# New addresses, 256-wide products, a fixed start order and the first head's rotation moved: a two-layer transformer trunk in split fp32

## The chip, the cores and the metric

The kernel runs on one core of a Trainium2 chip. The metric is the time of one execution on the device, in microseconds. Before the change it is 1125.92, the median of 3 runs (1125.34 to 1126.84).

## The reference, cut to what matters

Two trunk layers over 512 latent tokens of 1024 channels, with a context prefix of 256 tokens that only the first layer reads:

```python
for i in range(DEPTH):                                    # 2 layers
    sh1, sc1, g1, sh2, sc2, g2 = adaln_params(c, mod_w[i], mod_b[i])
    h = modulate(rms_norm(x, norm_g[i, 0]), sh1, sc1)
    if i % 2 == 0:    # 4 global heads (q and k normalised, rotated) and 4 windowed heads with a sink
        y, _ = attention_mixers(h, hc, w_in, w_out, q_g, k_g, sink, cos, sin, False)
    else:             # Fourier mixing over tokens and 4 groups of channels, then a linear map
        y = fourier_mix(h) @ fourier_w_out
    x = x + g1 * rms_norm(y, norm_g[i, 1])
    h = modulate(rms_norm(x, norm_g[i, 2]), sh2, sc2)
    x = x + g2 * rms_norm(conv_ffn(h, ...), norm_g[i, 3])   # d_ff = 2816, gated, depthwise conv of width 3
```

`adaln_params` is silu(c) times a 1024 x 6144 matrix. `apply_rope` multiplies each half of a head's channels by cosines and sines and adds them crosswise. Everything is float32.

## The kernel before, in words

**Numbers.** x stays transposed, [128 channels, 8 blocks of channels, 512 tokens]. A product in fp32 is made of three matmuls of type fp32r: each operand is split into a high part (ScalarE's copy to fp32r) and the rest (VectorE's subtraction), both on L127 in `split`. `mm3` then issues high x high (L104), high x low (L105) and low x high (L106). The pairs have two-letter names: `hh, hl` the modulated x, `wh, wl` a ring of five buffers for weights, `ch, cl` the context, `th, tl` the transposed probabilities, `qh, ql` a head's transposed queries, `xh, xl` and `zh, zl` the operands of the FFN and, in the helper `beside`, weights as well. `lhsT` is the operand held in the array as weights, `rhs` the one that moves through it, of 256 or 512 columns. `raw` is a ring of three buffers that DMAs on SyncE's queue fill.

**Addresses.** Each tile takes its bytes of a partition from a pool in the order of allocation, so a small tile ahead of another moves that one's address. `beside` puts 16 elements ahead of its weights and 16 behind.

**Order.** Work is written as Python code that calls generators (`pump(rest, n)` lets one advance by n steps); a scheduler orders the instructions of each engine by priority, which is the order of issue unless `later(n)` shifts it (a negative number is earlier). `follow(i, j)` fixes that i comes after j on its engine.

**The start (0 to 66.5 us).** The DMAs fill in the order in which they are issued: the first half of x, mod_s tile 0, constants, `w_kva` tile 0, mod_s tile 1, the second half of x, then the other tiles. The string `START` is the order in which the blocks are written: `M` (`mod_tile`) multiplies the conditioning vector by one of eight tiles mod_s and transposes the result; `W` splits weights; `X` sums squares of the second half of x; `F` (`feed`) normalises a block of x and multiplies it into the first projection of keys and values; `Y2`, `R2` normalise the context; `B0` is a filler, matmuls whose result nobody reads (`busy`, their numbers in `HOT`). The norm of the first half is spread inside `M0`, that of the second inside `M2`.

**Projections (66.5 to 112) and attention (112 to 255).** After `START` come three groups: `kb` and `vb` (the other keys and values, three blocks of tokens each) and `qa` (the queries of heads 0 and 1, two blocks). The other three groups of queries (`queries`, PSUM tile `gm`) are mixed into attention, `FILL` saying how many steps go where. `q_out` hands a block to `roped`, the rotation:

```python
def roped(dst, src, t0, gcol, stats=None, last=G):
    eng = V if gcol is None else last
    # squares on ScalarE; V: g = src * gqk; V: stats = reduce_sum(squares)
    # eng: t2 = crosswise src * sines, two halves (L814)
    # V: dst = src * cosines (L818);  last: dst = dst + t2 (L820)
```

`eng` and `last` are GpSimd for three query blocks of the first two groups; the block of heads 0 and 1 with the last tokens, (`qi == 0 and t0`), is on VectorE. The groups without a norm (`gcol is None`) multiply on VectorE and add on GpSimd. `queries_t` transposes a head's rotated queries (L998) and splits them; attention starts with `queries_t(0)`, and 12 steps of the next projection are placed behind it. GpSimd also normalises the probabilities P (L1053), which are transposed on L969.

**The rest.** Output projection (to about 318), first FFN (to 682), Fourier layer (to 765) and second FFN. Blocks of the FFNs in `SEVEN` are done by seven products of half size (256 columns), in `y_mm`; the other up projections (`up_mm`) and some of the down products are 512 wide.

Of the kernel before, what the change touches and what calls it, by code (L numbers as in the profile page):

```python
# [10 lines left out]
F32 = mybir.dt.float32  # L11
# [8 lines left out]
P = 128  # L20
# [32 lines left out]
SIDE = 16  # L53

WARM = 36
HOT = [5, 8, 5, 0]
# [3 lines left out]
START = ("M0 W0 X0 M1 B0 W1 F00 X1 F10 M2 F01 W2 F11 F20 M3 Y2 W3 F21 M4 R2 F30 F31 F02 W4 F12 F22 F32 M5 W5 F40 "  # L60
         "F41 M6 F42 W6 F50 F52 W7 F60 M7 F62 F51 F61 F70 F71 F72")
# [20 lines left out]
def kernel(ctx: ExitStack, tc: tile.TileContext, a):  # L82
# [17 lines left out]
    def f(ap):  # L100
        return ap.bitcast(F32)
# [24 lines left out]
    def split(h, l, src, eng=V):  # L126
        i = S.copy(out=h, in_=src), eng.tensor_tensor(out=l, in0=src, in1=f(h), op=ALU.subtract)  # L127
        for j in i:
            held(j)

# [8 lines left out]
    def wpair(shape):  # L139
        return mk(wp, shape, F32R, "wh", 5), mk(wp, shape, F32R, "wl", 5)  # L140
# [4 lines left out]
    con = mk(cp, [P, K_ALL], F32, "con")  # L145
    xT = mk(cp, [P, KC, T], F32, "xT")
    yT = mk(cp, [P, KC, T], F32, "yT")
    hh = mk(cp, [P, KC, T], F32R, "hh")
    hl = mk(cp, [P, KC, T], F32R, "hl")
    ident = con[:, K_ID:K_ID + P]  # L150
    ones32 = mk(cp, [P, 32], F32, "ones32")
    V.memset(ones32, 1.0)
    scol = mk(cp, [P, 2, KC], F32, "scol")
    eps = mk(cp, [P, 1], F32, "eps")
    once = mk(cp, [P, 1], F32, "once")
    mk(cp, [P, 8], F32, "cpad")
# [45 lines left out]
    def rstd(ps):  # L202
        w = ps.shape[1]
        v, t, r = (mk(cp, [P, W4], F32, "st_" + c, n)[:, :w] for c, n in (("v", 2), ("t", 1), ("r", 2)))
# [142 lines left out]
    class Plain:  # L347
# [5 lines left out]
        def tiles(self, ys, h, l, gi, pps, am, urgent=False, eng=None, pe=False):  # L353
            hs = halves[h]
            ps = ys.sums(pps, h)
# [10 lines left out]
            for k in range(KC):  # L366
# [5 lines left out]
                S.activation(out=hh[:, k, hs], in_=x, func=AF.Copy, scale=am[:, k:k + 1])  # L372
                V.scalar_tensor_tensor(out=hl[:, k, hs], in0=x, scalar=am[:, k:k + 1], in1=f(hh[:, k, hs]),  # L373
# [204 lines left out]
    with ExitStack() as es:  # L578
# [27 lines left out]
        with ExitStack() as e1:  # L606
# [30 lines left out]
            SY.dma_start(out=con, in_=a["con"])  # L637
# [29 lines left out]
            def mod_tile(c, mid=None):  # L667
# [8 lines left out]
                if mid is not None:  # L676
                    mid()
# [28 lines left out]

            ch = mk(pj, [P, KC, TC], F32R, "ch")
            cl = mk(pj, [P, KC, TC], F32R, "cl")

            tiles = [(hh, hl, t, 2 + t) for t in range(TT)] + [(ch, cl, t, t) for t in range(2)]  # L710
            sets = [(hh, hl, xT, halves[0]), (hh, hl, xT, halves[1]), (ch, cl, cT, slice(0, TC))]
# [4 lines left out]
            def feed(c, i):  # L716
# [5 lines left out]
                for n in range(2 * i, 2 * i + 2):  # L722
# [4 lines left out]
                    if (c, i) != (0, 1):  # L727
                        mm3(acc[n], sh[:, c, tk], sl[:, c, tk], wh[:, c % 2, :], wl[:, c % 2, :], c == 0, c == KC - 1)
                if (c, i) == (0, 1):

                    busy(warm, Rs[1], HOT[2])
                    for part in range(2):
                        for n in (2, 3):
                            sh, sl, t, b = tiles[n]
                            tk = slice(t * P, (t + 1) * P)
                            if part == 0:
                                PE.matmul(acc[n], lhsT=sh[:, c, tk], rhs=wh[:, 0, :], start=True, stop=False)
                                PE.matmul(acc[n], lhsT=sh[:, c, tk], rhs=wl[:, 0, :], start=False, stop=False)
                            else:
                                PE.matmul(acc[n], lhsT=sl[:, c, tk], rhs=wh[:, 0, :], start=False, stop=False)  # L740
                        if part == 0:
                            busy(warm, f(hh[:, 0, halves[1]]), HOT[3])

# [14 lines left out]

            for s in START.split():
                n = [int(c) for c in s[1:]]  # L760
                if s == "M0":
                    mod_tile(0, lambda: bcast(0, ps0))
                elif s == "M2":
                    mod_tile(2, lambda: bcast(1, Rs[1]))
                elif s == "Y2":
                    r2 = rstd(x_sums(cT, TC)[:, :W4])
                elif s == "R2":
                    Rs[2] = spread(r2, pps)
                elif s == "B0":
                    busy(warm, Rs[0], HOT[1])  # L770
                else:
                    {"M": mod_tile, "W": weights, "X": sums, "F": feed}[s[0]](*n)
# [23 lines left out]
            def roped(dst, src, t0, gcol, stats=None, last=G):  # L796
# [11 lines left out]
                if stats is not None:  # L808
                    V.reduce_sum(out=stats, in_=sq.rearrange("p (a d) -> p a d", d=P), axis=AX.X)
                t2 = mk(cp, [P, T], F32, "sq", 2).rearrange("p (t c) -> p t c", t=2)[:, :n, :]  # L810
# [9 lines left out]
                last.tensor_tensor(out=dst, in0=dst, in1=t2, op=ALU.add)  # L820

            kst = mk(pj, [P, 6, 2], F32, "kst")
# [51 lines left out]
            def q_out(qi, t0, ps):  # L874
                dst = Q[:, t0:t0 + 2, qi * 256:(qi + 1) * 256]
                if qi < 2:

                    roped(dst, ps, t0, 0, qst[:, qi, t0:t0 + 2, :].rearrange("p a b -> p (a b)"),
# [908 lines left out]
```

## Time and profile before

| | |
|---|---|
| time, median of 3 runs | 1125.92 us (1125.34 to 1126.84) |
| profiled execution | 1127.14 us, of which the profile's span is 1125.4 |
| mean clock granted to TensorE | 0.992 |
| TensorE busy (PE) | 1094.6 us, 97% of the span, 7798 matmuls |
| VectorE (DVE) | 901.9 us, 80% |
| ScalarE (ACT) | 593.6 us, 53% |
| GpSimd (POOL) | 148.9 us, 13% |
| DMA | 155.83 MB, mean 138 GB/s |

How to read the rows below. A row of instructions begins with the start in us from the span's start and the duration in us, then engine, line (that of the helper where one is used), operation, out<-in by the program's names, shapes and, after `x`, how many equal records the row covers. PE is the matmul, PEld the loading of its weights, which overlaps PE. A matmul's duration reaches to its modelled end and overlaps the next one's; the distance between two starts is the pace. A row of waits reads engine, tile and line that waited, `<-` what released it, then the sum in us, the count and the longest. In a group of instructions the three numbers after the count are the shortest, mean and longest in ns.

### The profile page before, as it was taken

The numbers are of one execution on the slowest core, as the hardware profiler recorded it, in microseconds if no ns is written. First come the engines' busy times: TensorE is split into PE (matmuls) and PEld (weight loads), VectorE is DVE, ScalarE is ACT, GpSimd is POOL, SyncE is SP. The second block draws the span as 40 slices with busy tenths as digits, with TensorE's granted clock in tenths as the row PEclk, the third lists the DMA queues.
The fourth block names the chain that finished last, engine by engine and source line by source line (L and its number), as shares of the span: only waits on it lengthen the run. The fifth ranks groups of instructions, "written<-read, shape, count | busy, mean of one in ns | idle before, by whom it ended". The sixth has DMA issues, their size and how long they took to land. (4 is left out here: it accounts for less than half of the span.)

```text
span 1125.4 us, 19521 instructions
## 1 busy us (share of the span) xinstructions
PE 1094.6 (97%) x7798; PEld 962.3 (86%) x7798; DVE 901.9 (80%) x1490; ACT 593.6 (53%) x1058; POOL 148.9 (13%) x161
## 2 busy tenths in 40 slices
PE   9999899999999999999999999989999999999995
PEld 5799888869898978887998998979888898899995
DVE  5788877764889966978999588878997998979756
ACT  4452456665675623552555445648745654655433
POOL 0047323412420000000000132400000000000012
PEclk9999999999999999999999998999999999999998
DMA  9775100172242465436525301921205523322332
GB/s 366 279 259 187 38 13 27 75 299 113 77 169 93 169 222 198 173 122 238 188 76 206 122 21 37 285 92 76 88 35 186 183 96 111 104 101 87 103 146 75
DMA packets 33763, 155.83 MB, mean 138 GB/s; under 512 B 3460, under 2 KB 8196, under 8 KB 22024
## 3 DMA queue, kind: packets, MB, share of 16 engines
q1 hardware_dynamic: 32520, 150.39, 36.9%
q0 software_dynamic: 1152, 4.19, 1.5%
q8 instruction: 61, 1.00, 0.4%
q14 instruction: 30, 0.25, 0.1%
HBM read 148.28 MB, written 6.29 MB: 137 GB/s over the span
## 5 line engine op out<-in xcount | busy, mean ns | idle before, releaser
L127 ACT CAST wh<-raw 128x1024 fp32r<-128x1024 f32 (+2 forms) x207 | 190.7, 932 | 165.1 <-PE mm L105 115.9
L127 DVE TENSOR_TENSOR wl<-raw,wh 128x1024 fp32r<-128x1024 f32 (+2 forms) x205 | 219.8, 1080 | 56.2 <-ACT wh L127 56.0
L104 PE MATMUL mm<-hh,wh 128*128 128x256 f32 (+1 forms) x632 | 204.3, 324 | 2.8 <-ACT sq L1224 1.2
L106 PE MATMUL mm<-hh,wl 128*128 128x256 f32 (+1 forms) x632 | 202.0, 320 | 0.4 <-DVE wl L127 0.2
L105 PE MATMUL mm<-hl,wh 128*128 128x256 f32 (+1 forms) x632 | 201.6, 319 | 0.0
L104 PEld LDWEIGHTS mm<-hh,wh 128*128 128x128 f32 x632 | 118.6, 188 | 17.5 <-ACT sq L1224 5.4
L106 PEld LDWEIGHTS mm<-hh,wl 128*128 128x128 f32 x632 | 118.6, 188 | 10.7 <-DVE wl L127 1.2
L105 PEld LDWEIGHTS mm<-hl,wh 128*128 128x128 f32 x632 | 118.7, 188 | 9.7
L292 POOL TENSOR_TENSOR gacc<-gacc,sq 128x256 f32<-128x256 f32 (+1 forms) x33 | 27.1, 820 | 720.3 <-ACT sq L290 717.6
L104 PE MATMUL mm<-zh,wh 128*128 128x256 f32 x384 | 109.5, 285 | 0.6 <-ACT sq L1222 0.6
L106 PE MATMUL mm<-zh,wl 128*128 128x256 f32 x384 | 107.1, 279 | 0.0
L105 PE MATMUL mm<-zl,wh 128*128 128x256 f32 x384 | 107.1, 279 | 0.0
L104 PE MATMUL mm<-xh,wh 128*128 128x512 f32 (+1 forms) x302 | 106.9, 354 | 0.0
L106 PE MATMUL mm<-xh,wl 128*128 128x512 f32 (+1 forms) x302 | 106.6, 353 | 0.0
L105 PE MATMUL mm<-xl,wh 128*128 128x512 f32 (+1 forms) x302 | 106.4, 352 | 0.0
L104 PEld LDWEIGHTS mm<-zh,wh 128*128 128x128 f32 x384 | 72.1, 188 | 4.8 <-ACT sq L1227 3.5
L106 PEld LDWEIGHTS mm<-zh,wl 128*128 128x128 f32 x384 | 72.5, 189 | 0.0
L105 PEld LDWEIGHTS mm<-zl,wh 128*128 128x128 f32 x384 | 72.1, 188 | 0.0
L104 PEld LDWEIGHTS mm<-xh,wh 128*128 128x128 f32 x302 | 56.7, 188 | 9.4 <-issue 1.6
L105 PEld LDWEIGHTS mm<-xl,wh 128*128 128x128 f32 x302 | 56.8, 188 | 8.4 <-issue 0.4
L106 PEld LDWEIGHTS mm<-xh,wl 128*128 128x128 f32 x302 | 56.8, 188 | 8.2
L1285 ACT ACTIVATE cv<-mm,cols 128x512 f32<-128x512 f32 x59 | 45.7, 777 | 22.3 <-PE mm L106 17.4
(432 smaller groups left out, 2759.3 us busy)
## 6 DMA issues: line engine op xcount, KB each, us to landing
raw<-in_w_up SPq DMA_DIRECT2D x42, 1024.0 KB, 4.9
xT<-in_mod_r SPq DMA_DIRECT2D x20, 1024.0 KB, 4.9
raw<-in_w_down SPq DMA_DIRECT2D x32, 384.0 KB, 3.0
raw<-in_mod_p SPq DMA_DIRECT2D x8, 1024.0 KB, 5.1
raw<-in_w_down SPq DMA_DIRECT2D x16, 512.0 KB, 3.8
raw<-in_w_in SPq DMA_DIRECT2D x6, 1024.0 KB, 7.1
yT<-in_mod_r SPq DMA_DIRECT2D x10, 512.0 KB, 5.0
raw<-in_w_out SPq DMA_DIRECT2D x4, 1024.0 KB, 6.0
```

The costliest lines, as they stand in the source:

```text
L104: i = PE.matmul(out, lhsT=ah, rhs=bh, start=start, stop=False, skip_group_check=skip)
L105: PE.matmul(out, lhsT=ah, rhs=bl, start=False, stop=False, skip_group_check=skip)
L106: return i, PE.matmul(out, lhsT=al, rhs=bh, start=False, stop=stop, skip_group_check=skip)
L127: i = S.copy(out=h, in_=src), eng.tensor_tensor(out=l, in0=src, in1=f(h), op=ALU.subtract)
L292: G.tensor_tensor(out=self.acc[:, sl], in0=self.acc[:, sl], in1=sq[:, sl], op=ALU.add)
L1285: S.activation(out=cv, in_=ps, func=AF.Identity, bias=bc, scale=wc[1])
```

## The change

- *Addresses.* New pads ahead of some tiles: `WPAD` ahead of the weights' ring, `CPAD` ahead of `ch`, `TPAD` ahead of `th`, `ZPAD` and others in the Fourier layer. `two` makes `hh` and `hl` 32 elements longer and gives a second view of the same memory, `hst, lst`, 128 bytes further on; that view is used where x is held as weights (the projections of `START` and attention, the Fourier layer's first product). `beside` now makes its buffers 1088 elements long. Small tiles move into `cols` and `con`, and `st_r` has one buffer instead of two.
- *256-wide products.* `y_mm` and `up_mm` do a 512-wide product as two halves of 256 columns, one after the other.
- *The start.* The second half of x is loaded ahead of mod_s tile 1. `START` has new steps: `T` is the transposing part of `M`, `Q1` and `R1` the norm of the second half, `R0` that of the first, `B1` a second place for fillers; TensorE's blocks are bound to that order. `HOT` goes from 8 and 5 fillers to 5 and 2.
- *The first head's rotation.* The block `qi == 0 and t0 == 2` gets priority, and the reduction of its squares and the splits of the next groups' weights follow its end. `queries_t(0)` comes behind five steps of the next projection, its third transpose bound behind them, and the splits of all heads' queries get priority.
- *GpSimd.* The rotation of the query blocks with a norm is wholly on VectorE.

The diff, cut:

```diff
-HOT = [5, 8, 5, 0]
+STAT = 32
+XW = 1088
+CPAD, TPAD, ZPAD, UPAD = 32, 32, 32, 56
+WPAD = 8
+HOT = [5, 5, 2]
-START = ("M0 W0 X0 M1 B0 W1 F00 X1 F10 M2 F01 W2 F11 F20 M3 Y2 W3 F21 M4 R2 F30 F31 F02 W4 ...
+START = ("M0 W0 R0 T0 B0 X0 W1 F00 X1 Q1 B1 M1 R1 T1 M2 F01 T2 F10 M3 F11 W2 T3 F20 Y2 M4 F21 T4 W3 F30 R2 ...
...
     def wpair(shape):
+        if (id(wp), "wh") not in nbufs:
+            mk(wp, [P, WPAD], F32, "wpad")
...
-    hh = mk(cp, [P, KC, T], F32R, "hh")
+    def two(tag):
+        t = mk(cp, [P, KC * T + STAT], F32R, tag)
+        return [t[:, o:o + KC * T].rearrange("p (k t) -> p k t", k=KC) for o in (0, STAT)]
+    hh, hst = two("hh")
+    hl, lst = two("hl")
...
             load_x(0)
             load_mod(0)
             load_kva(0)
+            load_x(1)
             load_mod(1)
-            load_x(1)
...
+                elif s == "Q1":
+                    Rs["r1"] = rstd(Rs[1][:, :W4])
+                elif s == "R1":
+                    Rs[1] = spread(Rs["r1"], pps)
+                elif s[0] == "B":
+                    busy(warm, Rs[0], HOT[1 + n[0]])
...
+                pe = [o for o in nc.cur_bb.bb.instructions[at:] if o.engine == mybir.EngineType.PE]
+                if pe:
+                    if done is not None:
+                        tc.add_manual_dep(pe[0], done, ... reason="order")
+                    done = pe[-1].name
...
     def roped(...):
-                last.tensor_tensor(out=dst, in0=dst, in1=t2, op=ALU.add)
+                end = last.tensor_tensor(out=dst, in0=dst, in1=t2, op=ALU.add)
+                if first:
+                    follow(V.reduce_sum(out=stats, in_=sq...), end)
+                    behind.append(end)
     def group_weights(g):
-                    split(wh, wl, r[:, 4 * i:4 * i + 4, :])
+                    j = split(wh, wl, r[:, 4 * i:4 * i + 4, :])[1]
+                    if behind:
+                        follow(j, behind[0])
     def q_out(qi, t0, ps):
-                    roped(dst, ps, t0, 0, qst..., V if qi == 0 and t0 else G)
+                    first = qi == 0 and t0 == 2
+                    with later(-10000 if first else 0):
+                        roped(dst, ps, t0, 0, qst..., V, first)
-            blocks = [(hh, hl, 0, 2), (hh, hl, 2, 4), (ch, cl, 0, 0)]
+            blocks = [(hst, lst, 0, 2), (hst, lst, 2, 4), (ch, cl, 0, 0)]
...
     def queries_t(head, behind=None):
+                    if behind is not None and j == 2:
+                        tc.add_manual_dep(i.ins, behind, ... reason="order")
-                split(qh, ql, pt)
+                with later(-10000):
+                    split(qh, ql, pt)
-            qh, ql = queries_t(0)
-            pump(rest, 12)
+            pump(rest, 5)
+            qh, ql = queries_t(0, [... last instruction on PE])
+            pump(rest, 7)
...
     def y_mm(pps, wts, movs, hs, last=True, ps=None):
-        for i in range(first, n + last):
-            mm3(ps[:, sl], wh, wl, bh[:, sl], bl[:, sl], i == 0, i == n)
+        for h in hs:
+            for i in range(first, n + last):
+                m.append(mm3(ps[:, halves[h]], wh, wl, bh[:, halves[h]], bl[:, halves[h]], ...))
     def beside(pool, shape, tag):
-        return mk(pool, [P, 2 * SIDE + n * m], F32R, tag, 4)[:, SIDE:SIDE + n * m]...
+        return mk(pool, [P, XW], F32R, tag, 4)[:, SIDE:SIDE + n * m]...
...
-                        up_mm(ps, w, slice(0, T))
+                        m = [up_mm(ps, w, s) for s in halves]
+                        follow(m[1][0][0], m[0][-1][1])
```

More of the change, by code (lines that the diff above doesn't have):

```diff
@@ L354, in tiles @@
             hs = halves[h]
+            vh, vl = (hh, hl) if pe else (hst, lst)
             ps = ys.sums(pps, h)
@@ L705, in x_sums @@
                 return ps
+            mk(pj, [P, CPAD], F32, "cpad")
             ch = mk(pj, [P, KC, TC], F32R, "ch")
             cl = mk(pj, [P, KC, TC], F32R, "cl")
-            tiles = [(hh, hl, t, 2 + t) for t in range(TT)] + [(ch, cl, t, t) for t in range(2)]
-            sets = [(hh, hl, xT, halves[0]), (hh, hl, xT, halves[1]), (ch, cl, cT, slice(0, TC))]
+            tiles = [(hst, lst, t, 2 + t) for t in range(TT)] + [(ch, cl, t, t) for t in range(2)]
+            sets = [(hst, lst, xT, halves[0]), (hst, lst, xT, halves[1]), (ch, cl, cT, slice(0, TC))]
             Rs = {}
@@ L721, in feed @@
                 wh, wl = kw[c // 2]
-                for n in range(2 * i, 2 * i + 2):
+                ns = range(2 * i, 2 * i + 2)
+                m = {}
+                for n in ns:
                     if c == 0:
@@ L726, in feed @@
                     tk = slice(t * P, (t + 1) * P)
[L727 to L742, printed above, removed]
+                    m[n] = acc[n], sh[:, c, tk], sl[:, c, tk], wh[:, c % 2, :], wl[:, c % 2, :]
+                if c == 0 and i < 2:
+                    for n in ns:
+                        ps, ah, al, bh, bl = m[n]
+                        PE.matmul(ps, lhsT=ah, rhs=bh, start=True, stop=False)
+                        PE.matmul(ps, lhsT=ah, rhs=bl, start=False, stop=False)
+                    for n in ns:
+                        ps, ah, al, bh, bl = m[n]
+                        PE.matmul(ps, lhsT=al, rhs=bh, start=False, stop=False)
+                else:
+                    for n in ns:
+                        mm3(*m[n], c == 0, c == KC - 1)
             def weights(c):
@@ L757, in bcast, with step @@
                 Rs[i] = stat_bcast(ps, pps)
-            for s in START.split():
[L760 to L772, printed above, removed]
+            def step(s):
+                n = [int(c) for c in s[1:]]
+                if s == "R0":
+                    bcast(0, ps0)
+                elif s == "Q1":
+                    Rs["r1"] = rstd(Rs[1][:, :W4])
+                elif s == "R1":
+                    Rs[1] = spread(Rs["r1"], pps)
+                elif s == "Y2":
+                    Rs["r2"] = rstd(x_sums(cT, TC)[:, :W4])
+                elif s == "R2":
+                    Rs[2] = spread(Rs["r2"], pps)
+                elif s[0] == "B":
+                    busy(warm, Rs[0], HOT[1 + n[0]])
+                else:
+                    {"M": mod_tile, "T": mod_turn, "W": weights, "X": sums, "F": feed}[s[0]](*n)
+            done = None
+            for s in START.split():
+                at = len(nc.cur_bb.bb.instructions)
+                step(s)
+                pe = [o for o in nc.cur_bb.bb.instructions[at:] if o.engine == mybir.EngineType.PE]
+                if pe:
+                    if done is not None:
+                        tc.add_manual_dep(pe[0], done, mybir.DependencyInfo(
+                            mybir.DependencyClass.NoSync, mybir.DependencyReason.DATA), reason="order")
+                    done = pe[-1].name
             S.activation(out=once, in_=modc[:, KC - 1, 0, 0:1], func=AF.Exp, scale=0.0)
@@ L794, with roped @@
             V.tensor_copy(out=identb, in_=ident)
-            def roped(dst, src, t0, gcol, stats=None, last=G):
+            def roped(dst, src, t0, gcol, stats=None, last=G, first=False):
                 n = src.shape[1]
@@ L876, in q_out @@
                 if qi < 2:
-                    roped(dst, ps, t0, 0, qst[:, qi, t0:t0 + 2, :].rearrange("p a b -> p (a b)"),
-                          V if qi == 0 and t0 else G)
+                    first = qi == 0 and t0 == 2
+                    with later(-10000 if first else 0):
+                        roped(dst, ps, t0, 0, qst[:, qi, t0:t0 + 2, :].rearrange("p a b -> p (a b)"), V, first)
                 else:
@@ L991, with queries_t @@
             pend = iter(())
-            def queries_t(head):
+            def queries_t(head, behind=None):
                 qh = mk(at, [P, T], F32R, "qh", 1)
@@ L1132, in spare_weights @@
         def spare_weights(self, shape):
-            return [beside(self.pool, shape, n) for n in ("zh", "zl")]
+            n, m = shape[1:]
+            o = SIDE if n * m + SIDE <= 1024 else 0
+            return [mk(self.pool, [P, 1024], F32R, t, 4)[:, o:o + n * m].rearrange("p (a b) -> p a b", b=m)
+                    for t in ("zh", "zl")]
     def up_weights(l, pairs, fis, eng=V):
```

74 lines of the change are left out of this document (44 added, 30 removed).

## The prediction

> **What bounds the kernel now.** I read the page's first part, then busy time by stage, then the waits of TensorE, then starts of single matmuls.
>
> ```profile
> span 1125.4 us, 19521 instructions
> PE 1094.6 (97%) x7798; PEld 962.3 (86%) x7798; DVE 901.9 (80%) x1490; ACT 593.6 (53%) x1058; POOL 148.9 (13%) x161
> ```
>
> ```profile
> core 0: us, PE busy (x) PEld busy (x) DVE busy (x) ACT busy (x) POOL busy (x), PEclk, DMA share, GB/s
> 0.00:66.50 66.50, 64.75 (x559) 43.97 (x560) 44.50 (x125) 33.45 (x73) 0.93 (x6) 1.00 0.81 309
> 112.00:255.00 143.00, 138.78 (x972) 119.10 (x971) 104.86 (x237) 82.13 (x167) 44.83 (x48) 1.00 0.24 89
> 360.00:640.00 280.00, 279.76 (x1681) 243.08 (x1681) 237.32 (x293) 137.13 (x205) 1.73 (x3) 1.00 0.48 171
> 640.00:682.00 42.00, 40.66 (x367) 39.15 (x366) 30.73 (x65) 19.68 (x46) 14.85 (x17) 0.96 0.10 34
> 682.00:765.00 83.00, 77.88 (x698) 69.83 (x700) 66.84 (x152) 47.90 (x108) 18.62 (x19) 0.96 0.49 159
> 850.00:1125.00 275.00, 262.20 (x1799) 237.82 (x1797) 220.83 (x302) 141.12 (x228) 12.63 (x16) 0.99 0.35 120
> ```
>
> The columns are the stretch, its length, then busy us and instructions of each engine. TensorE works 279.76 of 280 us in the first FFN, and almost without a break elsewhere. VectorE has 15% to spare there (237.32 of 280). So the end is set by how fast TensorE steps, and by the few places where it stands. A busy PE can still step slowly, so I read starts, not durations:
>
> ```profile
> 266.78 0.28 PE L104 MATMUL mm<-hh,xh 128*128 128x256 f32 x1
> 269.61 0.28 PE L104 MATMUL mm<-hh,xh 128*128 128x256 f32 x1
> 272.33 0.28 PE L104 MATMUL mm<-hh,xh 128*128 128x256 f32 x1
> ...
> 340.38 0.39 PE L104 MATMUL mm<-hh,wh 128*128 128x512 f32 x1
> 362.36 0.28 PE L104 MATMUL mm<-hh,wh 128*128 128x256 f32 x1
> ```
>
> Between the first two starts lie 24 equal matmuls: 2.83 us / 24 = 117.9 ns a step. Between the second and third lie 24 more of the same shape: 2.72 / 24 = 113.3 ns. There are two paces, 4.6 ns apart, and a run keeps its pace. The 512-column run steps (362.36 - 340.38) / 96 = 229.0 ns, between 2 x 113.3 = 226.6 and 2 x 117.9.
>
> Adding up the sizes of the tiles in the code gives the addresses: weights minus moving operand, modulo 256 bytes, is 192 in the slow run (hh at 0, weights at 192) and 64 in the next (hh at 0, weights at 64). It is no strict rule: the run that begins at 272.33 is at 192 again and stays at 113.3. After a break the distance decides more often than not. I went through the starts of the 256-wide three-product matmuls from attention's end on, 3,591 of them:
>
> ```profile
> 256.78 0.28 PE L104 MATMUL O<-th,wh 128*128 128x256 f32 x1
> 1112.77 0.28 PE L106 MATMUL mm<-xh,wl 128*128 128x256 f32 x1
> ```
>
> 3,400 of these step without a gap, at a mean of 116.6 ns; 70% are at the slow pace. Over all runs of 8 or more in the kernel that begin after a break, 52 lie at (moving 0, distance 192), and 91% of them start slow; 28 lie at (128, 64), and 36% do; 17 lie at (192, 64), 53%. At (0, 64) there are six runs, all fast, but only one of them after a break.
>
> **The change part by part.** Sums are made against the profiled execution, 1127.14 us (its span of 1125.4 and what lies around it); that is 1.2 above the median of 1125.92, and I take the 1.2 off at the end.
>
> *Addresses, and 512-wide products in halves.* The pads (WPAD 32 bytes, CPAD, STAT and the rest) and XW = 1088 (4352 bytes, a multiple of 256) put wh and wl at 64, hh, hl, xh, xl, zh at 0, weights held in xh at 64, and hst at 128: distance 64 nearly throughout, and (0, 64) in FFN and output projection. Excess over 113.3 now: 3,400 x 3.3 ns = 11.1 us in the 256-wide ones. The 512-wide ones number 1,451 from attention's end:
>
> ```profile
> 255.11 0.40 PE L105 MATMUL S<-hl,wh 128*128 128x512 f32 x1
> 1082.87 0.39 PE L106 MATMUL mm<-xh,wl 128*128 128x512 f32 x1
> ```
>
> They average 229.9, so their excess is 1,431 (those without a gap) x 3.3 = 4.7 us; together 15.8. Nearly all are now done as two halves: 3,591 + 2 x 1,451 = 6,493 steps. The halves cost nothing in themselves, since 2 x 113.3 is less than 229, and the doubled weight loads lie beside matmuls of the same width as those that already run at 113.3. At a slow share s the excess is 6,493 x 4.6 x s = 29.9 s us. Ends: s = 0 by the six runs at (0, 64) (-15.8), s = 0.70 as today (20.9, so +5.1). I take 0.2, between 0 and the 0.36 of (128, 64), nearest to the former as hh, xh and zh sit at 0 now: 6.0 left, 9.8 gained. VectorE must follow; with 15% spare against a TensorE that is 1% faster I let one tenth be lost: **-8.8** (+5.1 to -15.8).
>
> The Trainium skill (TensorE: Matmul & The Clock Gate, section "Step-by-step: what each phase is for") has it that the array reads its moving operand and its weights through two independent SBUF ports, so that loading the next weights takes nothing from the running matmul. By that rule no distance between the two could matter, and the sum would be that of the second rival below. The two runs of 117.9 and 113.3 ns speak against it as far as one changes with the distance, and the run from 272.33 on speaks for it.
>
> *The start.* The second half of x is loaded ahead of mod_s tile 1 on SP's queue, so that tile is later by 1 MB; at 309 GB/s that is 3.4 us. In the new order its products come behind F00, X1 and B1, later by about as much. The order of TensorE's blocks is written out, transposes T apart from M, and fillers drop from 8 + 5 to 5 + 2 matmuls.
>
> ```profile
> 13.01 2.13 PE L181 MATMUL mm<-Rs,ones 128*32 128x256 f32 x9
> 14.77 0.42 PE L672 MATMUL misc<-raw,spad 128*32 128x256 f32 x3
> 23.15 0.70 PE L233 MATMUL misc<-Rs,con 128*128 128x256 f32 x2
> 24.31 2.35 PE L181 MATMUL mm<-Rs,ones 128*32 128x256 f32 x10 [0.16 <-ACT Rs L234]
> 26.58 0.51 PE L737 MATMUL mm<-wh,hh 128*128 128x512 f32 x1
> ```
>
> Five fillers (ten records) take 2.35 us, 0.47 each: six fewer are 2.8 us. The 2.35 us at 24.31 stand where F01 waits for the spread of the second half's norm. With Q1 taken early, B1, M1, T1 and M2 fill that chain with real work. TensorE is otherwise busy up to 66.5, so what is saved reaches the end. Not all of it: F01's hh must still be made after R1. I take **-2.0**; ends +0.6 (all 3.4 us of the later load stand out, less 2.8 of fillers) and -4.0 (the fillers, and another 1.2 of the chain behind R1, from 23.15 to 24.31).
>
> *The first head.* After the last projection for head 0, TensorE reaches two transposes that wait for the rotated queries:
>
> ```profile
> PE PT L998 <- DVE yT L820: 1.7, 1, 1.7
> PE S L106 <- DVE ql L127: 1.2, 1, 1.2
> PE PT L969 <- POOL P L1053: 0.4, 2, 0.3
> ```
>
> ```profile
> 113.13 1.23 DVE L127 TENSOR_TENSOR wl<-raw,wh 128x1024 fp32r<-128x1024 f32 x1 [2.43 <-ACT wh L127]
> 114.27 0.68 DVE L804 TENSOR_TENSOR sq<-mm,Rs 128x512 f32<-128x512 f32 x1
> 114.87 0.67 DVE L809 TENSOR_REDUCE qst<-sq 128x4 f32<-128x512 f32 x1
> 115.47 0.68 DVE L818 TENSOR_TENSOR yT<-sq,gacc 128x512 f32<-128x512 f32 x1
> 116.06 0.75 DVE L814 TENSOR_TENSOR sq<-sq,gacc 128x256 f32<-128x256 f32 x2
> 116.81 1.22 DVE L127 TENSOR_TENSOR wl<-raw,wh 128x1024 fp32r<-128x1024 f32 x1
> 117.94 0.68 DVE L820 TENSOR_TENSOR yT<-yT,sq 128x512 f32<-128x512 f32 x1
> ```
>
> Two weight splits (1.23 and 1.22) and the reduction (0.67) stand in the rotation's way, which itself is 0.68 + 0.75 + 0.68 + 0.68 = 2.8 us. With the change these three go behind it: ready at about 116.1 instead of 118.6. The transposes are placed behind five more steps of the next projection (10 x 0.34 = 3.4 us of matmuls), at 116.8: no wait, 1.7 gained. The splits that go back are for weights used some 25 us later. The 1.2 us wait for ql is the same head's split, which now has priority: half of it. **-2.3** (0 to -2.9).
>
> *Rotations off GpSimd.* Three query blocks move two multiplications and the sum to VectorE.
>
> ```profile
> L814 DVE TENSOR_TENSOR sq<-gm,gacc x8: 411/414/425, 149.5 to 210.8; 128x256 f32<-128x256 f32 x8
> L820 DVE TENSOR_TENSOR yT<-yT,sq x1: 684/684/684, 117.9 to 117.9; 128x512 f32<-128x512 f32 x1
> L820 POOL TENSOR_TENSOR yT<-yT,sq x7: 1274/1293/1302, 111.4 to 212.0; 128x512 f32<-128x512 f32 x7
> ```
>
> That is 3 x (2 x 0.41 + 0.68) = 4.5 us more for VectorE, which is busy 104.86 of 143 us there (73%), so most of it lies beside matmuls; what is late next are splits that TensorE waits for. GpSimd's normalisation of P comes sooner, but TensorE waits for it 0.4 us only. (The sums of the last four query blocks stay on GpSimd, at 1.29.) I take **+0.5** (-0.4 to +4.5).
>
> The sum: -8.8 - 2.0 - 2.3 + 0.5 = -12.6; 1127.14 - 12.6 - 1.2 = **1113.3**. No row bears on the other edits (one st_r buffer instead of two, small tiles moved into cols and con): nothing.
>
> **The rivals.**
> 1. *All fast.* With every distance at 64 no run falls into the slow pace, s near 0.03: -0.9 x 14.9 = -13.4, and the start gives -4, the first head -2.9: -13.4 - 4 - 2.9 + 0.5 = -19.8, 1106. For it: the six runs at (0, 64), one taken up from a slow predecessor. Against: 36% of the runs at (128, 64) start slow.
> 2. *Distance is not the cause.* The pace is picked at a run's start by something else; the slow share stays 0.70, in the halves too: 29.9 x 0.70 = 20.9 against 15.8, +5.1, less the 4.3 of start and first head, plus 0.5: +1.3, 1127. For it: runs at 192 that are fast. Against: 91% slow at (0, 192), none at (0, 64).
> 3. *Slower: the halves.* Each 512-wide product at 229.9 becomes two 256-wide ones, and these lock into the slow pace, 235.8, as the 256-wide ones do. It decides from 29.9 s = 15.8 + 3.8 on, s = 0.66, where the kernel is as before; s = 0.85 gives 25.4 - 15.8 - 3.8 = +5.8, 1132; s = 1 gives 1136. For it: today's 70% in 256-wide runs. Against: that share is nearly all at distance 192 or right behind it.
>
> The clock is a further unknown: the two stretches at PEclk 0.96 hold spells at half clock, 42 x 0.04 = 1.7 us and 83 x 0.04 = 3.3 us lost; one such spell more or fewer moves the end by 1.7.
>
> **How the numbers follow.** Forecast 0.58, rival 1 0.20, rival 2 0.13, rival 3 0.09. A difference of 0.2% (2.3 us) is about what a measurement of this kernel tells from no change. Faster: forecast, rival 1 and a little of rival 2 (a start better than I take), 0.80. Same: most of rival 2, 0.11. Slower: rival 3, 0.09. The range of 8 in 10 goes from 1104 (rival 1 with one clock spell fewer) to 1125 (where rival 2 begins); the forecast's own is 1109 to 1118.
>
> **What would show it.** Right: starts in the FFNs 113 to 114 ns apart where they were 118, no 512-wide rows in the FFNs, the first FFN shorter by 3 to 5 us; the transposes' wait for L820's sum gone; the first block of the keys' and values' second projection before 66. Wrong: starts still 118 apart at distance 64 (rival 2 or 3); TensorE's waits for wl, tl or ql grown, which would mean that VectorE has become the bound; M1 standing behind its load.

## The result, and the profile after

| | before | changed |
|---|---|---|
| time, median | 1125.99 us (6 runs, 1125.34 to 1126.97) | 1119.03 us (6 runs, 1118.60 to 1121.77) |
| ratio | | 0.9943, interval 0.9932 to 0.9953 |
| profiled execution, span | 1127.14, 1125.4 | 1118.75, 1117.0 |

The change gains 0.57%, 6.4 us by the ratio, 7.0 by the medians. Forecast were 12.6 (1113.3 from 1125.92): right in sign and inside the wide range, but outside the forecast's own 1109 to 1118, and about twice too large.

Busy time by stage of the changed kernel, columns as in the prediction:

```profile
112.00:255.00 143.00, 140.43 (x980) 120.13 (x979) 105.60 (x244) 82.26 (x168) 38.45 (x41) 1.00 0.23 89
360.00:640.00 280.00, 278.42 (x2396) 272.19 (x2395) 234.09 (x289) 135.90 (x205) 2.44 (x4) 1.00 0.48 173
682.00:765.00 83.00, 77.79 (x716) 69.04 (x716) 66.80 (x156) 46.37 (x105) 18.16 (x19) 0.98 0.49 159
```

The halves are there (2396 matmuls in the first FFN instead of 1681), and in attention GpSimd has 38.45 us where it had 44.83. In the Fourier layer the clock is 0.98 where it was 0.96: one spell at half clock fewer, 83 x 0.02 = 1.7 us. The prediction named that as a further unknown; it is part of this execution's gain and not of the change's design.

The pace, by starts:

```profile
314.11 0.28 PE L108 MATMUL mm<-hh,xh 128*128 128x256 f32 x1
361.45 0.28 PE L108 MATMUL mm<-hh,wh 128*128 128x256 f32 x1
...
866.04 0.28 PE L108 MATMUL mm<-zh,wh 128*128 128x256 f32 x1
882.93 0.28 PE L108 MATMUL mm<-zh,wh 128*128 128x256 f32 x1
```

402 matmuls lie between the first two starts, 117.8 ns each; 149 between the others, 113.3. By the addresses added up from the code both runs are at moving 0, distance 64, so the slow pace exists there too. From attention's end on 28% of the gapless 256-wide steps are slow instead of 70%.

I then took every matmul record after attention (the same columns in all these kernels), and added up by how much the distance to the next start exceeds 113.3 ns per 256 columns. Up to 13% over counts as pace, more as a break (a wait, or the restart beside a matmul of another kind). The Fourier layer's 258-wide products are counted too, so "before" is a little more than the prediction's 15.8:

| kernel | attention ends, us | pace excess after it, us | breaks after it, us |
|---|---|---|---|
| before | 262.6 | 17.1 | 41.1 |
| changed | 260.6 | 10.3 | 43.6 |
| halves alone | 263.4 | 22.2 | 43.2 |
| addresses alone | 263.5 | 16.9 | 43.3 |
| addresses and halves | 263.1 | 7.3 | 51.2 |

Attention ends 2.0 us sooner; after it the pace gives 6.8, breaks take 2.5, and matmuls outside the products take 2.0 less (1.7 of it the spell at half clock). That is the 8.4 by which the span is shorter.

The same sums by FFN show where the pace went. The first FFN goes here from the last spread of a norm ahead of it to the next spread (rows of before, then of the changed kernel), the second from the last spread ahead of it to the last matmul:

```profile
316.94 0.70 PE L233 MATMUL misc<-Rs,con 128*128 128x256 f32 x2
656.24 0.67 PE L233 MATMUL misc<-Rs,con 128*128 128x256 f32 x2
```

```profile
313.45 0.70 PE L244 MATMUL misc<-Rs,con 128*128 128x256 f32 x2
653.28 0.70 PE L244 MATMUL misc<-Rs,con 128*128 128x256 f32 x2
```

| us: length, pace excess, breaks | first FFN | second FFN |
|---|---|---|
| before | 339.3, 6.5, 6.9 | 338.7, 6.9, 13.1 |
| changed | 339.8, 5.1, 8.8 | 334.9, 1.6, 14.7 |
| halves alone | 344.9, 9.6, 9.5 | 341.7, 8.9, 14.1 |
| addresses and halves | 340.1, 2.4, 11.8 | 337.0, 1.3, 17.0 |

The first FFN is no shorter than before: breaks eat what the pace gains. The second is 3.8 us shorter.

### The profile page after: what moved, and what is told of

It is laid out like the page before. It is cut to its first block, busy times and chain, and to the rows that moved or that the text cites. A ratio compares the mean times of both kernels' runs of the same rounds, so it can differ in the third digit from the quotient of the medians.

```text
span 1117.0 us, 22365 instructions
## 1 busy us (share of the span) xinstructions
PE 1085.8 (97%) x9220; PEld 1014.8 (91%) x9220; DVE 902.2 (81%) x1499; ACT 593.4 (53%) x1058; POOL 140.6 (13%) x152
## 5 line engine op out<-in xcount | busy, mean ns | idle before, releaser
L108 PE MATMUL mm<-hh,wh 128*128 128x256 f32 x856 | 240.7, 281 | 2.2 <-ACT sq L1273 1.4
L110 PE MATMUL mm<-hh,wl 128*128 128x256 f32 x856 | 238.0, 278 | 2.1 <-DVE wl L131 2.1
L109 PE MATMUL mm<-hl,wh 128*128 128x256 f32 x856 | 237.8, 278 | 0.0
L108 PEld LDWEIGHTS mm<-hh,wh 128*128 128x128 f32 x856 | 161.0, 188 | 7.0 <-ACT sq L1273 5.9
L110 PEld LDWEIGHTS mm<-hh,wl 128*128 128x128 f32 x856 | 160.7, 188 | 2.9 <-DVE wl L131 2.5
L109 PEld LDWEIGHTS mm<-hl,wh 128*128 128x128 f32 x856 | 161.4, 189 | 0.3 <-DVE hl L263 0.2
L108 PE MATMUL mm<-xh,wh 128*128 128x256 f32 x492 | 137.6, 280 | 0.0
L110 PE MATMUL mm<-xh,wl 128*128 128x256 f32 x492 | 136.7, 278 | 0.0
L109 PE MATMUL mm<-xl,wh 128*128 128x256 f32 x492 | 136.7, 278 | 0.0
L108 PEld LDWEIGHTS mm<-xh,wh 128*128 128x128 f32 x492 | 92.7, 188 | 2.3 <-issue 2.1
L1334 ACT ACTIVATE cv<-mm,cols 128x512 f32<-128x512 f32 x59 | 45.9, 778 | 13.1 <-PE mm L110 8.1
```

Of the source, the lines that this page charges most:

```text
L108: i = PE.matmul(out, lhsT=ah, rhs=bh, start=start, stop=False, skip_group_check=skip)
L109: PE.matmul(out, lhsT=ah, rhs=bl, start=False, stop=False, skip_group_check=skip)
L110: return i, PE.matmul(out, lhsT=al, rhs=bh, start=False, stop=stop, skip_group_check=skip)
L1334: S.activation(out=cv, in_=ps, func=AF.Identity, bias=bc, scale=wc[1])
```

## The experiments

"Before" was run beside each group; ratios are to it. Medians differ by some 1 us from group to group, so ratios are compared.

| run | what it is | median, us | ratio (interval) |
|---|---|---|---|
| e1 | before + start + first head | 1123.39 | 0.9970 (0.9958 to 0.9981) |
| e15 | before + start | 1126.51 | 0.9999 (0.9987 to 1.0011) |
| e2 | before + addresses | 1128.25 | 1.0007 (0.9998 to 1.0015) |
| e3 | before + halves | 1134.66 | 1.0069 (1.0056 to 1.0082) |
| e4 | before + addresses + halves | 1125.08 | 0.9982 (0.9971 to 0.9992) |
| e5 | changed, without halves | 1124.74 | 0.9981 (0.9971 to 0.9992) |
| e6 | changed, evictions first | 1119.55 | 0.9934 (0.9918 to 0.9950) |
| e7 | changed, matmuls behind spreads | 1123.72 | 0.9974 (0.9963 to 0.9985) |
| e8 | changed, splits on GpSimd | 1138.34 | 1.0098 (1.0079 to 1.0117) |
| e9 | before, 35 sums cut | 1128.59 | 1.0021 (1.0012 to 1.0029) |
| e10 | e3, 35 sums cut | 1136.91 | 1.0088 (1.0074 to 1.0101) |
| e11 | e4, 35 sums cut | 1123.95 | 0.9976 (0.9967 to 0.9985) |
| e12 | changed, 35 sums cut | 1121.95 | 0.9958 (0.9945 to 0.9970) |
| e13 | changed, inputs later | 1119.44 | 0.9931 (0.9917 to 0.9944) |
| e14 | changed, inputs on GpSimd | 1127.21 | 1.0002 (0.9991 to 1.0014) |
| e16 | e4, inputs' sums cut | 1123.65 | 0.9966 (0.9954 to 0.9977) |
| e17 | before, inputs' sums cut | 1125.97 | 0.9984 (0.9976 to 0.9993) |
| e18 | e6 and e13 together | 1118.66 | 0.9929 (0.9912 to 0.9945) |

**The parts of the change** (each hunk of the diff belongs to one of four parts; these kernels have some of them).

e1, start and first head:

> Kernel before with the new start and the first head's rotation (queries without GpSimd, priorities, queries_t behind five steps) and nothing else: old addresses, 512-wide products whole. By the two traces attention ends 2.0 us sooner in the changed kernel, so theory A (the parts add up) expects -2.0, 1124. By the terms of the prediction it would be -2.0 - 2.3 + 0.5 = -3.8, 1122. Rival: the changed trace is 2.0 ahead by its addresses in attention's projections, and these parts alone give nothing: 1126.

e15, the start alone:

> Kernel before with the new start alone (load order, order of blocks, fewer fillers). Prediction's term -2.0. By the traces the first block of the next projection begins 0.9 us sooner in the changed kernel, so -0.9: 2.8 us of fillers saved, 1.6 lost again in slower and more broken 512-wide products. What start and first head gave together was -3.3, so the first head would be -2.4 by the one, -1.3 by the other.

e2, addresses alone:

```diff
+    hh, hst = two("hh")        # with all pads and views; y_mm and up_mm as before
```

> Kernel before with the new addresses alone; 512-wide products stay whole, old start, old first head. Theory A (the distance between weights and moving operand decides how often a run locks into the slow pace, 28% of steps slow at 64): the 256-wide steps go from 11.1 us of excess to 3,400 x 4.6 ns x 0.28 = 4.4, that is -6.7. The 512-wide ones are the question: in the changed kernel's start they step at 233.4 ns instead of 232.1, so at distance 64 they may cost 1,431 x (233.4 - 229.9) = +5.0; sum -1.7, 1124. Rival B (distance is not the cause): no change, 1126, and the slow share of 256-wide steps stays at 0.70.

e3, halves alone:

```diff
+        for h in hs:           # y_mm and up_mm in halves; hh, hl and all addresses as before
```

> Kernel before with the 512-wide products in halves alone, at the old addresses. Theory A: at distance 192 the new 256-wide steps are slow as the old ones are, 0.70 of 6,493 steps x 4.6 ns = 20.9 us against 15.8 now: +5, 1131. Rival B (the halves are what makes the pace fast, addresses do nothing): -6, 1120.

e4, both:

> Kernel before with new addresses and halves, old start and old first head. Theory A: what the changed kernel shows after attention, -4.3 in the steps of the products (7.0 less of slow pace, 2.7 more in gaps), and if its shorter wait of 2.3 at the beginning of the Fourier layer belongs to this part, -6.3: 1120 to 1122. By the prediction's term -8.8, 1117. Rival: the parts do not add up, because the pace of each long run is drawn anew at the break before it; then 1117 to 1124 with slow runs in other places than in the changed kernel.

e5, the changed kernel with `y_mm` and `up_mm` as before:

> The changed kernel with its 512-wide products whole again. Theory A (parts add: start and head -3.3 as in the run of these alone, addresses alone +0.8): -2.5 against before, so about 4 slower than the changed kernel; the 512-wide steps at 233 ns (9.5 us of excess) as in the run of addresses alone. Rival (what the halves gain in pace comes back as waits for evictions, since two halves leave VectorE and ScalarE less time): as fast as the changed kernel, -6.

Start and first head give -3.4 us, as good as all of it by the first head: the start alone gives -0.1. e5 came as theory A said: without the halves the changed kernel is 4.3 us slower, its 512-wide excess 9.4. Halves at the old addresses cost 7.8 us: the third rival's mechanism, which the addresses prevent. Addresses alone give nothing, for a reason I had not seen, the 512-wide products:

```profile
342.00 0.39 PE L108 MATMUL mm<-hh,wh 128*128 128x512 f32 x1
349.69 0.39 PE L108 MATMUL mm<-hh,wh 128*128 128x512 f32 x1
```

In this timeline of e2, 33 matmuls take 233.2 ns each, and 98% of the 512-wide steps are slow; the excess of the 256-wide ones (without the Fourier layer's 258-wide) falls from 11.1 to 6.0 us, that of the 512-wide ones rises from 4.8 to 9.5. So addresses and halves belong together. But together they give only -2.0 (interval -0.9 to -3.3) for 9.8 us of pace. The waits of TensorE in the FFNs (windows 320 to 660 and 760 to 1090), for before and for e4:

```profile
PE mm L106 <- DVE wl L127: 0.2, 1, 0.2
...
PE mm L104 <- ACT sq L1224: 1.2, 2, 1.0
PE mm L104 <- ACT sq L1222: 0.6, 1, 0.6
PE mm L104 <- DVE sq L1284: 0.2, 1, 0.2
```

```profile
PE mm L108 <- ACT sq L1246: 1.3, 4, 0.5
PE mm L108 <- ACT sq L1249: 1.2, 1, 1.2
PE mm L108 <- ACT sq L1244: 1.1, 2, 0.8
PE misc L493 <- DVE gacc L455: 0.2, 1, 0.2
...
PE mm L110 <- DVE wl L131: 2.0, 2, 1.4
PE mm L108 <- ACT sq L1246: 1.7, 3, 1.0
PE mm L108 <- ACT sq L1249: 1.2, 1, 1.2
PE mm L108 <- ACT sq L1244: 0.3, 1, 0.3
```

2.2 us became 9.0 (`sq` are evictions inside the seven products, `wl` weight splits). By the starts, the steps from product to product that hold a wait of over 0.15 us are 8.2 us longer in output projection and FFNs. Not all of that comes from the pace: with halves alone, at the slow pace, the same waits are 5.3 us too, and the breaks in the two FFNs 3.6 us longer than before (in e4 8.8). In the changed kernel the waits are 4.2, and it keeps more.

**Whose lateness?** Two theories: C, evictions stand behind casts in ScalarE's queue; D, VectorE is late. One of e4's waits, engine by engine, shows how the two can be links of one chain:

```profile
992.71 1.22 DVE L131 TENSOR_TENSOR wl<-raw,wh 128x1024 fp32r<-128x1024 f32 x1
993.95 0.33 SPq L140 DMA_DIRECT2D raw<-in_w_up  x1
999.45 0.62 ACT L131 CAST wh<-raw 128x512 fp32r<-128x512 f32 x1 [1.42 <-DMA raw<-in_w_up]
999.97 0.37 ACT L1246 COPY sq<-mm 128x256 f32<-128x256 f32 x1
1000.39 0.39 PE L108 MATMUL mm<-hh,wh 128*128 128x256 f32 x1 [0.96 <-ACT sq L1246]
```

A split on VectorE frees a `raw` buffer, the DMA into it begins and lands 5.5 us later, ScalarE's cast has waited for it, the eviction stands behind the cast, and TensorE waits 0.96 us for the eviction. Of e4's twelve waits of over 0.25 us, five (3.3 of 8.5 us) hang in this way on a cast that waits for a DMA. No run changes the FFNs' loads or the number of `raw` buffers.

e6, the four copies of `seven_products` with priority:

```diff
-        S.copy(out=xs[:, :HT], in_=y[:, HT:])
+        with later(-10000):
+            S.copy(out=xs[:, :HT], in_=y[:, HT:])
```

> The changed kernel with the four evictions by ScalarE inside each seven_products given priority over the splits. Theory C (the pace gained is given back where TensorE waits inside the seven products for an eviction that stands behind a cast of weights on ScalarE: 1.8 us in the changed kernel's profile, 6.8 in that of addresses and halves alone): these waits fall under 1 us, the time by 1 to 3 us. Rival D (ScalarE's order is not it; VectorE's splits and sums come too late, and what TensorE does not wait for at an eviction it waits for at wl): the same total of waits, time within 1 us.

The waits in the FFNs went from 4.2 to 5.4 us, the ratio is 1.0 us under the changed kernel's, inside both intervals. That does not settle C. In ScalarE's order the edit moves only four of them: from 320 on, 49 of the 96 `sq` evictions in e6 stand right behind a cast, 47 in the changed kernel.

e7, two more matmuls in `spread` after attention:

```diff
+            for _ in range(2):
+                j = PE.matmul(R[:32, HT:HT + 64], lhsT=ones32, rhs=Rs[:, :64], start=True, stop=True)
```

> The changed kernel with two matmuls of 64 columns (ones times the tile just spread, nobody reads them) behind each spread of a norm after attention. In the changed kernel all seven breaks by a spread with a gap of 192 ns are followed by the slow pace (420 steps from 314 on, 160 from 653 on, 90 from 1093 on), nine of nine breaks by a matmul with ones by the fast one. Theory C: the run from 314 on becomes fast, TensorE reaches the first seven products 1.9 us sooner and waits there; slow share from 0.28 to 0.18, time only 0 to -1.5. Rival (TensorE's pace alone sets the time): -3.3 for 720 steps x 4.6 ns, less 0.5 for the added matmuls: -2.8.

A miss: 3.5 us slower than the changed kernel. The spread that cost 420 slow steps in the changed kernel is this:

```profile
313.45 0.70 PE L244 MATMUL misc<-Rs,con 128*128 128x256 f32 x2
313.80 0.47 PE L110 MATMUL mm<-hh,xl 128*128 128x256 f32 x1
314.11 0.28 PE L108 MATMUL mm<-hh,xh 128*128 128x256 f32 x1
```

The matmul behind it takes 306 ns to the next start, 192 more than its pace. With the added matmuls that step is 113 too long, and the 420 steps are slow all the same (slow share 0.30 against 0.28). In the eleven kernels with new addresses and halves, 483 of 570 runs behind a step too long by 106 to 110 ns begin at the fast pace, none of 74 behind one of 112 to 114, and 15 of 59 behind one of 192: the pace goes with a few ns of the break, and I could not set it. The matmuls outside the products take 34.6 us instead of 28.5, which is far more than the 0.5 that I allowed, 1.7 of it by a third spell at half clock.

e8, 17 weight splits to GpSimd:

```diff
-                split(wh, wl, r[:, i, :, :], eng)
+                split(wh, wl, r[:, i, :, :], G if i and late else eng)
```

> The changed kernel with half of the weight splits of the up projections outside the seven products (17 subtractions of 1.22 us) on GpSimd, which is idle in the FFNs. Theory D (VectorE is what is late next): 20 us less on VectorE, waits in the FFNs under 1 us, time -1 to -3. Theory C (ScalarE's order): no change. Rival: GpSimd needs some 2.5 us for each (twice as long as VectorE's, by 1.29 against 0.68 us for the sum in the rotation) and TensorE then waits for wl: +1 to +5.

e14, two of the four inputs of the seven products to GpSimd:

```diff
-            split(*b[n], src)
+            split(*b[n], src, G if n in "47" else V)
```

> The changed kernel; of the four inputs of the seven products that are split in each FFN, the two used last (4 and 7) have their subtraction on GpSimd: 2 x 1.24 us less on VectorE in each of the two stretches where it is busy without a break (340 to 375, 813 to 830). Theory D: -1 to -3, the wait for wl at 827 gone. Rival (GpSimd's 2.5 to 3.8 us for each, as in the run with weight splits on it, is too slow, or slows VectorE beside it): 0 to +4, with waits for zl or slower VectorE rows there.

Both go the rival's way, and further than it said: 17.5 and 6.6 us above the changed kernel. One reason is in VectorE's rows of e14, GpSimd's first:

```profile
824.61 5.60 POOL L131 TENSOR_TENSOR zl<-yT,zh 128x1024 fp32r<-128x1024 f32 x2 [92.75 <-ACT zh L131]
...
823.98 1.21 DVE L131 TENSOR_TENSOR zl<-yT,zh 128x1024 fp32r<-128x1024 f32 x1
825.11 2.89 DVE L131 TENSOR_TENSOR xl<-cv,xh 128x512 fp32r<-128x512 f32 x1
827.92 3.38 DVE L131 TENSOR_TENSOR wl<-raw,wh 128x1024 fp32r<-128x1024 f32 x1
```

While GpSimd splits, VectorE's next splits take 2.89 and 3.38 us instead of 0.7 and 1.2: the two work one after the other. The Trainium skill (SBUF — State Buffer, section "Who interferes with whom") says so: a VectorE instruction with two SBUF inputs contends with a GpSimd instruction that reads SBUF, and what they contend for is an exclusive lock. The trace agrees. In e14 two spells at half clock inside the FFNs, 3.4 us long each, add some 3.4 us.

e9 to e12, 35 of VectorE's sums in the first FFN over 64 of 1024 columns, in four kernels:

```diff
-    held(V.scalar_tensor_tensor(out=acc, in0=w[:, i, :], scalar=scol[:, 0, k:k + 1], in1=acc, ...
+    held(V.scalar_tensor_tensor(out=acc[:, :64], in0=w[:, i, :64], scalar=scol[:, 0, k:k + 1], in1=acc[:, :64], ...
```

> Kernel before, where 35 of VectorE's sums in the first FFN (1.28 us each, 45 us in all, from 330 to 577; the next layer's modulation) run over 64 of 1024 columns; the rest of these sums is left out. Theory D (VectorE is what is late next when TensorE's pace rises): the kernel before has a slow pace there and few waits, so it gains 0 to -1.5. Theory C (the waits inside the seven products come from ScalarE's order): 0.

> The kernel with halves alone (old addresses, slow pace), with the same 35 sums cut to 64 columns. Theory D: -1 to -3 against the run of halves alone (gap excess in output projection and first FFN 18.4, of which some 2.5 are waits that the kernel before has not), 1132. Theory C: no change, 1134.7.

> The kernel with addresses and halves alone (fast pace), with the same 35 sums cut to 64 columns. In output projection and first FFN its pace excess is 3.5 us against 7.8 before, its gaps 20.9 against 15.9. Theory D: with VectorE light the gaps fall to 16 or less, so -4 to -6 against the run without the cut, 1120, and the difference to the halves at old addresses grows from 9.6 to 12 or 13. Theory C: the gaps stay, 1124 to 1125.

> The changed kernel with the same 35 sums cut to 64 columns. Its gaps there are 16.3 us at a pace excess of 6.5. Theory D: -1 to -4 against the changed kernel, 1116, more where the long run from 314 on happens to be fast. Theory C: no change, 1119.

VectorE is busy 31 us less (e9 870.8 us, before 901.9). In the first FFN the waits of e4 fell from 3.8 to 1.3 us, those of e3 and of the changed kernel stayed (2.3 and 2.4, 1.2 and 1.3), those of before rose from 0.2 to 1.1, and no time came of it. By the ratios e11 is 0.7 us under e4, the other three are 1.7 to 2.4 us over their likes; why less work costs time is not known. That is not what D expected; how much VectorE has to do in all is not the cause.

**The full stretches.** VectorE by stretch, in the kernel before and in e4:

```profile
340.00:375.00 35.00, 34.77 (x200) 30.23 (x200) 35.00 (x45) 19.11 (x28) 0.00 (x0) 1.00 0.23 91
780.00:830.00 50.00, 49.84 (x240) 41.62 (x239) 48.81 (x85) 36.40 (x56) 0.00 (x0) 1.00 0.18 64
```

```profile
340.00:375.00 35.00, 33.03 (x287) 32.45 (x286) 35.00 (x45) 17.78 (x26) 0.00 (x0) 1.00 0.25 91
780.00:830.00 50.00, 49.86 (x437) 49.65 (x437) 50.00 (x86) 36.58 (x56) 0.00 (x0) 1.00 0.18 64
```

Where the inputs of the seven products are made, VectorE (the third pair) is busy 35.00 of 35 and 48.8 to 50.0 of 50 us, before as well. In the changed kernel one sees a wait that comes of it: VectorE's rows, then TensorE's.

```profile
822.21 1.23 DVE L131 TENSOR_TENSOR zl<-yT,zh 128x1024 fp32r<-128x1024 f32 x1
823.34 0.75 DVE L1335 SCALAR_TENSOR_TENSOR cv<-mm,cols,cv 128x511 f32<-128x511 f32 x1
824.00 1.22 DVE L131 TENSOR_TENSOR zl<-yT,zh 128x1024 fp32r<-128x1024 f32 x1
825.13 0.75 DVE L1337 SCALAR_TENSOR_TENSOR cv<-mm,cols,cv 128x511 f32<-128x511 f32 x1
825.79 2.36 DVE L131 TENSOR_TENSOR wl<-raw,wh 128x1024 fp32r<-128x1024 f32 x2
...
827.07 0.38 PE L110 MATMUL mm<-hh,wl 128*128 128x256 f32 x1 [1.39 <-DVE wl L131]
```

TensorE waits 1.39 us for the first of the two splits `wl`, which stands behind two inputs `zl` of products that begin later.

e13, in the second FFN the inputs one pair of blocks later:

```diff
-SUMS = [5, 7]
+SUMS = [5, 8]
```

> The changed kernel; in the second FFN the inputs of the seven products (four sums and four splits of 1.24 us on VectorE) are made one pair of blocks later, behind the weight splits of that pair. In the changed kernel VectorE is busy 17.00 of 17 us there (813 to 830) and TensorE waits 1.39 us for a split wl behind them. Theory D (in these stretches VectorE sets the time, so pace gained there is given back): the wait goes, and as the next weights come ahead of the inputs, -0.5 to -1.5, 1118. Rival: the inputs are then late for the first seven products, the wait moves there: 0 to +2.

e16 and e17, the four sums of `seven_inputs` over 16 of 256 columns, in e4 and in the kernel before:

```diff
+        b11, b12, b21, b22 = (v[:, :, :16] for v in full)
```

> The kernel with addresses and halves alone; the four sums that make the inputs of the seven products (1.24 us each, in each FFN) run over 16 of 256 columns, the rest is left out: some 4.5 us less on VectorE in each of the two full stretches. Theory D: -2 to -5 against the run without the cut (1125.1), waits of over 0.5 us outside the Fourier layer from 10.0 us to under 6. Rival (the waits come from somewhere else, and each run draws them anew): within 1.5 of 1125.

> Kernel before with the same sums cut. Theory D: at the slow pace VectorE is as full there (35.00 of 35, 48.8 of 50 us), but TensorE waits only 3.0 us in waits of over 0.5: 0 to -2, less than in the kernel with the fast pace. Rival: the same gain as there.

e18:

> The changed kernel with both edits, evictions first and the second FFN's inputs of the seven products one pair later. Each alone gave 0.9934 and 0.9931 of before, the changed kernel 0.9943. If they add up: 0.992, 1117 to 1118; if each only draws the waits anew: 0.993 to 0.9945.

e13: the wait of 1.39 us is gone, but the waits for evictions grow, and the sum in the FFNs goes from 4.2 to 6.7 us. e16: the waits in the FFNs are 4.8 us where e4 has 9.0, the time is 1.8 us less than e4's (the intervals of both are +-1.3). e17: 2.2 to 1.1 us of waits, and -1.8 us too (0.8 to 2.7). This does not show D. The edit did not empty the stretches: in e16 VectorE is still busy 34.77 of 35 and 50.00 of 50 us. And each sum of waits is from one execution: e4 and the changed kernel, whose work on these engines is the same there, differ by as much (9.0 and 4.2). In time the fast pace gains no more than the slow one, as the rival said. e13 and e18 have the lowest ratios of all, 1.4 and 1.6 us under the changed kernel's, inside both intervals: no better version is shown.

**What stays open.** That breaks grow where the pace rises is measured. Row by row it is shown that single waits come from VectorE's full stretches (1.39 us at 827) and from casts that wait for a DMA (0.96 us at 1000); how the whole divides between these, and why halves raise the waits at the slow pace too, is not settled. Neither is why e4 waits 9.0 us and the changed kernel 4.2. From the output projection on the two have the same instructions in the same order on TensorE, ScalarE and VectorE, at the same addresses; they reach it 2.5 us apart and end 7 apart. Which runs of matmuls are slow, and which waits follow, differs between them, and e4's own runs spread from 1122.6 to 1127.5.

## Why the prediction was right or wrong

*Addresses and halves, -8.8: wrong, by the give-back.* The pace came nearly as forecast: at a slow share of 0.2 I had an excess of 6.0 in place of 15.8; e4 has 5.9 at 0.18, the changed kernel 8.8 at 0.28 (again without the 258-wide), so there 2.8 of the 9.8 us are missing by the share alone. The step that failed is "with 15% spare against a TensorE that is 1% faster I let one tenth be lost". Lost is far more: in e4 the breaks grow by 10.1 us against 9.8 of pace gained, and from e1's trace to the changed kernel's by 3.1 (40.5 to 43.6) against 6.6 (16.9 to 10.3). The 15% is a mean over 280 us; in the two stretches above nothing is spare, and the evictions hang on ScalarE's order and on DMAs, which the step did not consider. Which of them makes how much of it is open. Measured: -2.0 alone, -3.0 as the difference between the changed kernel's ratio and e1's. That the halves "cost nothing in themselves" is wrong too: e3's excess is 5.1 larger, as I had it for s = 0.70, but its time 7.8, and part of e4's breaks comes with the halves (3.6 us in the FFNs in e3).

*The second rival (distance is not the cause): fell.* Halves without and with the new addresses are at slow shares of 0.72 and 0.18. So the addresses matter; that it is the distance modulo 256 bytes and not, say, the place of the weights alone, which the pads move with it, no run separates. The rule of the Trainium skill that was quoted there (TensorE: Matmul & The Clock Gate, section "Step-by-step: what each phase is for") makes no room for that; the measurement decides.

*The first rival (all fast): fell.* In the eleven kernels with new addresses and halves 35% of 864 runs behind a break start slow, about the 36% of (128, 64), not the none of the six runs that I put first.

*The start, -2.0: wrong.*

```profile
17.91 0.81 PE L192 MATMUL mm<-Rs,ones 128*32 128x256 f32 x3
20.07 0.67 PE L244 MATMUL misc<-Rs,con 128*128 128x256 f32 x2 [0.26 <-DVE Rs L241]
21.20 1.07 PE L686 MATMUL misc<-yT,spad 128*32 128x256 f32 x16 [0.24 <-ACT Rs L245]
24.17 0.44 PE L695 MATMUL misc<-con,sq 128*128 128x128 f32 x2 [0.25 <-ACT sq L689]
```

The 2.8 us of fillers are saved, but new waits stand between the blocks (1.6 us in all where there were 0.4, the longest 0.6 for `ch`), and the 512-wide products lose 1.6 us in breaks and pace: the next projection begins 0.9 sooner, as the next row shows (66.47 before), and 0.6 of that is lost to slower steps by 113.

```profile
65.59 0.28 PE L108 MATMUL mm<-wh,hh 128*128 128x256 f32 x1
```

Alone it gave 0 (+-1.3): in e15 the next projection begins 0.7 sooner, and the slower steps behind it take 0.6 of that too. I had counted the chain behind R1 once and not the restarts of five blocks.

*The first head and the rotations, -2.3 + 0.5: right, rather small.* Changed kernel, VectorE and then TensorE's waits from 112 to 255:

```profile
115.98 0.69 DVE L848 TENSOR_TENSOR yT<-yT,sqx 128x512 f32<-128x512 f32 x1
116.59 0.68 DVE L850 TENSOR_REDUCE qst<-sq 128x4 f32<-128x512 f32 x1
117.19 1.22 DVE L131 TENSOR_TENSOR wl<-raw,wh 128x1024 fp32r<-128x1024 f32 x1
```

```profile
PE gm L108 <- DVE sq L832: 0.8, 1, 0.8
PE S L110 <- DVE ql L131: 0.7, 1, 0.7
```

The sum of the rotation ends at 116.67 instead of 118.62, the transposes' wait of 1.7 is gone, the reduction and the splits stand behind it, and the wait for `ql` fell from 1.2 to 0.7: the steps as written. What I had not listed is 0.8 for `gm`. The term was -1.8; e1 less e15 is -3.3. In their traces attention ends 1.6 us sooner (262.6 and 261.0), which is about the term; the rest lies in shorter breaks after it (43.0 and 40.5), which I had no reason to expect.

*The signs.* No 512-wide product is left in the FFNs, the transposes' wait is gone and the first block of the second projection begins before 66, as written. The first FFN was to be 3 to 5 us shorter and is 0.5 longer; the second gained instead. Of the signs of being wrong, the wait for `wl` grew from 0.2 to 2.1 us and some starts at distance 64 are still 118 apart.

*The sum.* Of -12.6, the -8.8 was lost for two thirds or more and the -2.0 wasn't there. By luck the first head's part came out larger than its steps, and in the profiled execution one spell at half clock fewer hid some of the loss.

## What to carry to other kernels

Mean spare time of the next engine says little about a gain of 1%: look at its busy time in stretches of the length of one tile's chain, and follow what TensorE waits for there back through every engine and load of the chain, before counting gained pace as gained time. Sum pace and breaks by stage: one FFN may keep the gain and the other lose it. An experiment meant to empty a full stretch, or to change an order, is to be checked for having done so. Changes that help only together (here addresses and halves) must be summed together, and priced alone each may be nothing or a loss. In e14, work that left VectorE for GpSimd did not run beside VectorE's two-input splits.

## What I had not expected of the hardware

The same new addresses that make 256-wide products mostly fast make 98% of the 512-wide ones slow (233 ns against 229.9 at the old addresses). The pace after a break goes with few ns of the break's length. And TensorE's clock falls to half inside an FFN, where it was 1.00 before: in e8 for 3.4 us behind a wait of 3.8 (at 367) and for 6.8 us behind one of 2.8 (at 474), though not behind waits of 3.8 and 3.4 us (at 844 and 861). e8's waits and clock:

```profile
PE mm L108 <- ACT sq L1271: 10.3, 4, 3.8
...
355.00:380.00 25.00, 21.13 (x165) 20.56 (x164) 24.40 (x31) 14.43 (x23) 1.24 (x1) 0.93 0.35 117
```
